# A hybrid decoder trunk: the same tiles, laid out so that the large ones begin at multiples of 1024 bytes

## The chip, the cores and the metric

The kernel runs on one core of a Trainium2 chip. The metric is the device time of one execution in microseconds (us). Before the change the median of three runs is 1990.35 us (1989.92 to 1994.62). PE is the matrix engine (PEld its weight loads), DVE the vector engine, ACT the scalar engine, POOL the GpSimd, SP the queue that issues the transfers. SBUF is the on-chip memory of 128 partitions that all tiles below live in; the matmul results go to eight banks of PSUM.

## The reference

A two-layer trunk on x (256 tokens, 2048 features), all in float32:

```python
x = recurrent_block(x, norm1_g[0], lru_w_in[0], conv, gates, lambda, lru_w_out[0])   # RMSNorm, 2048 -> 4096, conv, RG-LRU scan, 2048 -> 2048
x = swiglu_ffn(x, norm2_g[0], ffn_w_in[0], ffn_w_out[0])      # 2048 -> 2 x 5632 -> 2048
k_band, v_band = shared_kv(x, kv_norm_g, w_kv, k_norm_g)      # 4 heads of 64
x = attn_block(x, norm1_g[1], w_q[0], q_norm_g[0], sinks[0], w_o[0], k_band, v_band)   # 32 heads, window 128, sinks
x = swiglu_ffn(x, norm2_g[1], ffn_w_in[1], ffn_w_out[1])
```

All the work that counts is in the projections: some 373 MB of float32 weights are read once, each multiplied with 256 token columns.

## The kernel before, in words

**A product in three.** Every float32 operand is split into a high part (rounded to the matrix engine's fp32r format) and a low part, the rest. A product is then high x high, high x low and low x high, each an fp32r matmul. The weights are loaded from HBM in tiles of 128 x 1024 floats (512 KB) into one of four buffers `raw`, ACT copies the rounded part into `hi` (L311) and DVE subtracts it from `raw` into `lo` (L312); `hi` and `lo` have four buffers each as well. The activations x are kept transposed, and their high and low parts lie side by side in one work tile of the pool `s`, 256 high columns and then 256 low ones: a half of one of thirty 4096-byte tiles `s0` to `s29`, handed out and taken back by the class itself.

**The order of the work.** `stream` (L332) goes through a list of jobs, one for each weight tile: it issues the load of the tile four jobs ahead, splits the tile three jobs ahead, and records the matmuls of the job itself. Between the halves of a job, background tasks (norms, convolution, scan, attention, splitting of activations) are recorded as far as a budget of DVE and ACT time goes, which is kept in constants of the class and not in anything that is measured or that depends on where a tile lies.

**Which operands meet in the matrix engine.** A matmul has a stationary operand, which is loaded first (128 columns), and a moving one that is streamed through it (256 or 512 columns of 4 bytes). A profile names a matmul `out<-moving,stationary`.
- L358 (`products`), the bulk: stationary is 128 columns of `hi` or `lo`, moving 256 columns of an `s` tile (`b<-s,hi`, `b<-s,lo`). In some jobs (`sync`) a few are 512 columns wide, the high and the low part at once.
- L512 (`put`, in the groups of the feed-forward input with an odd number from 5 to 17), where pairs of products are replaced by seven products of sums: a job of `fast` has seven triples of matmuls. In three triples (9 matmuls) the moving operand is a weight tile, `hi` or `lo`, and the stationary one an activation in `s` (`b<-hi,s`, `b<-lo,s`). In the other four (12 matmuls) the moving operand is a sum of weights, made by `mix` (L314) into tiles of the pool `s`, so that both operands are in `s` (`b<-s,s`). Jobs of `plain` have moving operands in `hi` and `lo` alone.

The two lines of `fast` that say which operand is where, and the order of the triples:

```python
old = lambda q: (hi[:, q * T:q * T + T], lo[:, q * T:q * T + T])
new = lambda q: (mh[:, q * T:q * T + T], ml[:, q * T:q * T + T])
todo = ((5, part(a, 0), old(1)), (3, part(b, 0), old(3)), (2, com(3), old(2)),
        (7, com(0), new(0)), (6, com(2), new(1)), (4, com(1), new(2)), (1, part(b, 1), new(3)))
```

- L1232 (queries): stationary `s`, moving 512 columns of `hi` or `lo`. L1274: thirty matmuls on a tile of zeros at the start, while the first weights are still on their way.

**Where a tile lies.** A pool places its tiles one behind the other in the order in which they are first asked for, each rounded up to 32 bytes. `par` (1096 bytes a partition), `con` (4104) and `cc` (128) come first; x, `raw`, `hi`, `lo` and the small tiles follow, and the thirty `s` tiles, asked for last, come behind `rstd` (1032 bytes each), `acc`, `sq` and `zero`. So x, `raw`, `hi`, `lo`, `t` and `h` all begin 384 bytes past a multiple of 1024, and the `s` tiles 960 past one, that is 64 bytes short of the next. A second pool, `tmp`, holds `nm`, `nt`, `r2` and `rr`.

Of the kernel before, what the change touches and what calls it, by code (L numbers as in the profile page):

```python
# [12 lines left out]
F32 = mybir.dt.float32  # L13
F32R = mybir.dt.float32r
# [3 lines left out]
P = 128  # L18
D = 2048
T = 256  # L20
# [15 lines left out]
K_ONE, K_BLK, K_SEL0, K_SEL1, K_ID = 0, 128, 256, 384, 512  # L36
K_HS, K_MASK = 640, 642
NCON = 642 + 384


class Val:


    def __init__(self, ap=None):
        self.ap = ap
        self.ready = False


class Trunk:
# [22 lines left out]
    def __init__(self, ctx, tc, dram):  # L72
        self.tc, self.nc, self.d = tc, tc.nc, dram
        nc = self.nc
        const = ctx.enter_context(tc.tile_pool(name="const", bufs=1))
        psum = ctx.enter_context(tc.tile_pool(name="psum", bufs=1, space=bass.MemoryType.PSUM))
        tmp = ctx.enter_context(tc.tile_pool(name="tmp", bufs=1))
        self.tmp = tmp
        self.par = const.tile([P, NPAR], F32, name="par")
        self.con = const.tile([P, NCON], F32, name="con")  # L80
        self.cc = const.tile([P, 32], F32, name="cc")
        self.x = [const.tile([P, 4, T], F32, name=f"x{i}") for i in range(4)]
        self.whole = deque((i, 0) for i in range(30))
        self.stamp = 0
        self.part = {F32: deque(), F32R: deque()}
        self.spool = const
        self.held = {}
        self.raw = [const.tile([P, 1024], F32, name=f"raw{i}") for i in range(4)]
        self.hi = [const.tile([P, 1024], F32R, name=f"hi{i}") for i in range(4)]
        self.lo = [const.tile([P, 1024], F32R, name=f"lo{i}") for i in range(4)]  # L90
        self.sets = [[psum.tile([P, 512], F32, name=f"b{4 * i + j}") for j in range(4)] for i in range(2)]
        self.banks = deque(b for q in self.sets for b in q)
        self.misc = 0
        self.started = False
        self.tmps = deque(const.tile([P, T], F32, name=f"t{i}") for i in range(4))
        self.halves = deque(const.tile([P, T], F32, name=f"h{i}") for i in range(4))
        self.rstd = [const.tile([P, T + 2], F32, name=f"rstd{i}") for i in range(2)]
        self.acc = const.tile([P, T], F32, name="acc")
        self.sq = deque(const.tile([P, T], F32, name=f"sq{i}") for i in range(2))
        self.zero = const.tile([P, P + T], F32R, name="zero")  # L100
        self.jobs = []
        self.mixed = {}
        self.pend = deque()
        self.bg = deque()
        self.tick = -2 * self.LD
        self.dve = 0.0
        self.act = 0.0
# [1141 lines left out]

    def run(self):  # L1250
        nc, d = self.nc, self.d
        const = self.tmp
        self.nm = const.tile([P, T + 2], F32, name="nm")
        self.nt = const.tile([P, T + 2], F32, name="nt")
        self.r2 = const.tile([P, 2], F32, name="r2")
        self.rrs = [const.tile([P, 48], F32, name=f"rr{i}") for i in range(2)]
        self.rv = {i: Val() for i in range(4)}
        self.rstd = {0: self.rstd[0], 1: self.rstd[1], 2: self.rstd[0], 3: self.rstd[1]}
        vals = lambda: [Val() for _ in range(ND)]
        self.xs0, x1, xk, x2, x3 = (vals() for _ in range(5))  # L1260

        def first():
            for k in range(ND):
                self.gained(k, [(C_N1A, self.xs0)])
                yield 2 * (k == 1)
            for k in range(ND):
                yield from self.squares(k)
            yield from self.norm(0, self.NORM0)
            self.decay()
        self.spawn(first())  # L1270
        nc.vector.memset(self.zero[:, :].bitcast(F32), 0.0)
        p = self.bank()
        for _ in range(self.WARM):
            nc.tensor.matmul(p[:, 0:T], self.zero[:, 0:P], self.zero[:, P:P + T], start=True, stop=True)  # L1274
        self.free_bank(p)

        self.lru([(C_N2A, x1)], 1)
        self.ffn(0, x1, 1, [(C_KVG, xk)], 2, C_N2A)
        self.kv(xk, 2, [(C_N1B, x2)])
        self.attn(x2, 2, [(C_N2B, x3)], 3)  # L1280
        self.ffn(1, x3, 3, None, None, C_N2B, d["out"])
        self.stream()
# [14 lines left out]
def constants():  # L1297
    i = np.arange(P)
    con = np.zeros((P, NCON), np.float32)
    con[:, K_ONE:K_ONE + P] = 1.0  # L1300
# [46 lines left out]
```

## Time and profile before

| | us |
|---|---|
| median of 3 runs (lowest, highest) | 1990.35 (1989.92, 1994.62) |
| the profiled execution | 1994.55 |
| its span, first to last instruction | 1992.4 |
| PE busy | 1982.9 (16487 matmuls) |
| DVE busy | 1458.5 (2319 instructions) |
| ACT busy | 1123.0 (1626 instructions) |
| DMA, share of its 16 engines (weights, x, output) | 56.6% |

The profile is of one execution. The end of a matmul is modelled, and matmuls overlap, so the busy time of PE says that it never stands still, and not how fast it goes. How fast it goes is read from a count and a stretch: so many matmuls between two starts. The timeline and the chain of waits both give a start, a length and a count in each row.

### The profile page before, as it was taken

The page shows a single profiled execution, that of the slowest core. Times are in us where ns is not written, and L with a number is a line of the kernel's source. Part 1 is how long each engine was busy: PE and PEld are TensorE (multiplying, and loading weights), DVE is VectorE, ACT ScalarE, POOL GpSimd, SP SyncE. Part 2 cuts the span into 40 slices and gives each one's busy share as a digit, 9 for nine tenths or more (in the row PEclk, how much of TensorE's full clock was granted, in tenths as well). Part 3 has the DMA queues.
Part 4 walks back from the last instruction along what each step waited for, and adds up shares of the span by engine and source line. Part 5 has one row for each costly group of instructions (what it writes and reads, how often), then busy time and mean ns, then how long its engine had stood idle before and what let it go on. Part 6 is the DMA issues. An engine that isn't in the chain of part 4 may idle for free. (4 is left out here: it accounts for less than half of the span.)

```text
span 1992.4 us, 39949 instructions
## 1 busy us (share of the span) xinstructions
PE 1982.9 (100%) x16487; PEld 1935.5 (97%) x16487; DVE 1458.5 (73%) x2319; ACT 1123.0 (56%) x1626; POOL 0.2 (0%) x4
## 2 busy tenths in 40 slices
PE   9999999999999999999999999999999999999999
PEld 9999999999999999999998789999999999999999
DVE  8989868788888955555677776697888888444543
ACT  7788756555555744444556775564555556444342
POOL 0000000000000000000000000000000000000000
PEclk9999999999999999999999999999999999999999
DMA  7555655655566565555554334565655655556663
GB/s 267 194 188 180 201 191 180 202 198 194 199 201 199 196 196 197 191 191 201 192 181 154 111 128 150 189 191 190 203 201 196 198 196 197 187 190 204 208 202 128
DMA packets 105015, 376.56 MB, mean 189 GB/s; under 512 B 11648, under 2 KB 13824, under 8 KB 104832
## 3 DMA queue, kind: packets, MB, share of 16 engines
q1 hardware_dynamic: 104544, 373.60, 56.6%
q8 instruction: 129, 2.11, 0.4%
q14 instruction: 54, 0.44, 0.1%
q10 hardware_dynamic: 288, 0.40, 0.1%
HBM read 371.86 MB, written 2.10 MB: 188 GB/s over the span
## 5 line engine op out<-in xcount | busy, mean ns | idle before, releaser
L358 PE MATMUL b<-s,hi 128*128 128x256 f32 (+1 forms) x8455 | 1128.5, 280 | 1.6 <-ACT s L118 1.2
L312 DVE TENSOR_TENSOR lo<-raw,hi 128x1024 fp32r<-128x1024 f32 (+1 forms) x621 | 755.9, 1220 | 435.7 <-ACT hi L311 421.2
L358 PEld LDWEIGHTS b<-s,hi 128*128 128x128 f32 x8455 | 1051.7, 188 | 14.2 <-ACT s L118 2.0
L311 ACT ACTIVATE hi<-raw 128x1024 fp32r<-128x1024 f32 (+1 forms) x621 | 654.2, 1056 | 590.5 <-PE b L358 475.0
L358 PE MATMUL b<-s,lo 128*128 128x256 f32 x4352 | 647.1, 277 | 0.0
L358 PEld LDWEIGHTS b<-s,lo 128*128 128x128 f32 x4352 | 564.7, 188 | 0.1
L512 PE MATMUL b<-hi,s 128*128 128x256 f32 (+1 forms) x868 | 163.0, 292 | 0.0
L325 ACT ACTIVATE s<-s 128x1024 fp32r<-128x1024 f32 x84 | 89.2, 1062 | 108.6 <-DVE s L324 107.8
L512 PEld LDWEIGHTS b<-hi,s 128*128 128x128 f32 x868 | 130.4, 189 | 3.8
L512 PE MATMUL b<-s,s 128*128 128x256 f32 x1008 | 133.3, 281 | 0.0
L512 PEld LDWEIGHTS b<-s,s 128*128 128x128 f32 x1008 | 125.2, 189 | 0.0
L327 DVE TENSOR_TENSOR s<-s,s 128x1024 fp32r<-128x1024 f32 x84 | 102.7, 1222 | 20.1 <-ACT s L325 19.9
L512 PE MATMUL b<-lo,s 128*128 128x256 f32 (+1 forms) x434 | 114.1, 289 | 0.0
L118 ACT ACTIVATE s<-s 128x512 fp32r<-128x512 f32 (+3 forms) x172 | 83.0, 519 | 18.4 <-DVE s L127 13.1
L321 ACT ACTIVATE hi<-raw 128x768 fp32r<-128x768 f32 x84 | 70.3, 843 | 35.1 <-issue 21.8
L1232 PE MATMUL b<-hi,s 128*128 128x512 f32 x256 | 84.0, 408 | 0.0
L326 DVE TENSOR_TENSOR lo<-raw,hi 128x768 fp32r<-128x768 f32 x84 | 79.9, 951 | 0.0
L512 PEld LDWEIGHTS b<-lo,s 128*128 128x128 f32 x434 | 76.4, 188 | 1.8
L127 DVE TENSOR_TENSOR s<-s,s 128x512 fp32r<-128x512 f32 (+2 forms) x143 | 74.0, 549 | 4.4 <-ACT s L118 4.4
L322 DVE TENSOR_TENSOR s<-raw 128x512 f32<-128x512 f32 x84 | 57.7, 686 | 12.4 <-DMA raw<-in_ffn_in 12.3
L118 ACT ACTIVATE s<-b 128x256 fp32r<-128x256 f32 (+4 forms) x112 | 49.9, 480 | 25.9 <-PE b L1128 7.9
L1232 PEld LDWEIGHTS b<-hi,s 128*128 128x128 f32 x256 | 45.8, 189 | 9.6 <-issue 1.4
(117 smaller groups left out, 1098.6 us busy)
## 6 DMA issues: line engine op xcount, KB each, us to landing
raw<-in_ffn_in SPq DMA_DIRECT2D x352, 512.0 KB, 3.3
raw<-in_ffn_out SPq DMA_DIRECT2D x176, 512.0 KB, 3.3
raw<-in_lru_in SPq DMA_DIRECT2D x63, 512.0 KB, 3.8
raw<-in_lru_out SPq DMA_DIRECT2D x32, 512.0 KB, 3.4
raw<-in_w_q SPq DMA_DIRECT2D x32, 512.0 KB, 3.2
raw<-in_w_o SPq DMA_DIRECT2D x32, 512.0 KB, 3.3
raw<-in_gate SPq DMA_DIRECT2D x8, 512.0 KB, 4.0
raw<-in_kv SPq DMA_DIRECT2D x8, 512.0 KB, 3.2
```

What stands on the lines that cost most here:

```text
L118: self.nc.scalar.activation(out, in_, func, **kw)
L127: self.nc.vector.tensor_tensor(out, a, b, op)
L311: self.nc.scalar.activation(hi[:, q], raw[:, q], AF.Copy)
L312: self.nc.vector.tensor_tensor(lo[:, q], raw[:, q], hi[:, q].bitcast(F32), ALU.subtract)
L321: act(hi[:, q], raw[:, q], AF.Copy)
L322: tt(two(d[:, 0:2 * T]), two(raw[:, T:3 * T]), raw[:, 0:T].unsqueeze(1).to_broadcast([P, 2, T]), ALU.subtract)
L325: act(mh[:, :], d[:, :], AF.Copy)
L326: tt(lo[:, q], raw[:, q], hi[:, q].bitcast(F32), ALU.subtract)
L327: tt(ml[:, :], d[:, :], mh[:, :].bitcast(F32), ALU.subtract)
L358: self.nc.tensor.matmul(ps[f][:, 0:c1 - c0], w, x2[k][:, c0:c1], start=f not in begun, stop=last and all(q[1] != f for q in todo[n + 1:]))
L512: nc.tensor.matmul(st["ps"][b][:, h % 2 * T:(h % 2 + n) * T], x, w, start=b not in st["begun"], stop=True, skip_group_check=True)
L1232: nc.tensor.matmul(st[g][b][:, :], x, q, start=c + kt == 0 and x is xh and q is wh, stop=c == 7 and kt == 1 and q is wl)
```

## The change: the order in which the tiles are allotted

Nothing is computed differently. The small tables (`rstd`, `nm`, `nt`, `r2`, `rr`, `zero`) are asked for directly behind `par`, `con` and `cc`, then a pad of 608 bytes that nobody reads or writes, then x, `raw`, `hi`, `lo` and the work tiles, and the `s` tiles last as before. The pool `tmp` is gone, its tiles are in `const`. `acc` is now the first of three tiles of one list.

```diff
+PAD = 152
...
-        tmp = ctx.enter_context(tc.tile_pool(name="tmp", bufs=1))
-        self.tmp = tmp
...
         self.cc = const.tile([P, 32], F32, name="cc")
+        self.rstd = [const.tile([P, T + 2], F32, name=f"rstd{i}") for i in range(2)]
+        self.nm, self.nt = (const.tile([P, T + 2], F32, name=n) for n in ("nm", "nt"))
+        self.r2 = const.tile([P, 2], F32, name="r2")
+        self.rrs = [const.tile([P, 48], F32, name=f"rr{i}") for i in range(2)]
+        self.zero = const.tile([P, P + T], F32R, name="zero")
+        const.tile([P, PAD], F32, name="pad")
         self.x = [const.tile([P, 4, T], F32, name=f"x{i}") for i in range(4)]
+        self.raw = [const.tile([P, 1024], F32, name=f"raw{i}") for i in range(4)]
+        self.hi = [const.tile([P, 1024], F32R, name=f"hi{i}") for i in range(4)]
+        self.lo = [const.tile([P, 1024], F32R, name=f"lo{i}") for i in range(4)]
+        self.tmps = deque(const.tile([P, T], F32, name=f"t{i}") for i in range(4))
+        self.halves = deque(const.tile([P, T], F32, name=f"h{i}") for i in range(4))
+        self.sq = deque(const.tile([P, T], F32, name=f"sq{i}") for i in range(3))
+        self.acc = self.sq.popleft()
```

Byte addresses within a partition, and what they leave on division by 1024 and by 512:

| tiles | first address before | mod 1024 | mod 512 | first address after | mod 1024 | mod 512 |
|---|---|---|---|---|---|---|
| `x0` to `x3` | 21888 | 384 | 384 | 28672 | 0 | 0 |
| `raw0` to `raw3` | 38272 | 384 | 384 | 45056 | 0 | 0 |
| `hi0` to `hi3` | 54656 | 384 | 384 | 61440 | 0 | 0 |
| `lo0` to `lo3` | 71040 | 384 | 384 | 77824 | 0 | 0 |
| `t`, `h` (eight of 1024 bytes) | 87424 | 384 | 384 | 94208 | 0 | 0 |
| `acc`, `sq` | 97728 | 448 | 448 | 102400 | 0 | 0 |
| `s0` to `s29` | 102336 | 960 | 448 | 105472 | 0 | 0 |
| `rstd` | 95616 | 384 | 384 | 21888 | 384 | 384 |
| `zero` | 100800 | 448 | 448 | 26528 | 928 | 416 |

`par`, `con` and `cc` stay where they were. The instructions of every engine and of every queue, their order and what each waits for are the same, row for row: 10864 rows of PE, 2230 of DVE, 1513 of ACT and 715 of SP in both programs. What differs is the address in an operand, the line numbers, and the name `sq` where `acc` stood.

More of the change, by code (lines that the diff above doesn't have):

```diff
@@ L87, in __init__ @@
         self.held = {}
-        self.raw = [const.tile([P, 1024], F32, name=f"raw{i}") for i in range(4)]
-        self.hi = [const.tile([P, 1024], F32R, name=f"hi{i}") for i in range(4)]
-        self.lo = [const.tile([P, 1024], F32R, name=f"lo{i}") for i in range(4)]
         self.sets = [[psum.tile([P, 512], F32, name=f"b{4 * i + j}") for j in range(4)] for i in range(2)]
@@ L94, in __init__ @@
         self.started = False
[L95 to L100, printed above, removed]
         self.jobs = []
@@ L1251, in run @@
         nc, d = self.nc, self.d
[L1252 to L1256, printed above, removed]
         self.rv = {i: Val() for i in range(4)}
```

## The prediction

> **What bounds the kernel now.** I read the page's busy times first, then what the matrix engine waits for, then the chain of waits.
>
> ```profile
> PE 1982.9 (100%) x16487; PEld 1935.5 (97%) x16487; DVE 1458.5 (73%) x2319; ACT 1123.0 (56%) x1626; POOL 0.2 (0%) x4
> ...
> PE b L463 <- DVE acc L127: 1.7, 1, 1.7
> PE b L1274 <- DVE zero L1271: 1.3, 1, 1.3
> PE b L358 <- ACT s L118: 1.2, 2, 0.8
> ...
> core 0: 1992.4 us, clock 1.000
> ```
>
> PE is never without work: its three longest waits come to 4.2 us of a span of 1992.4, at a full granted clock. DVE and ACT are idle for a quarter and for nearly a half of it. So the time is 16487 matmuls one behind the other, and only the distance from one matmul to the next can move it. The mean length of a matmul is modelled and says little about that distance; a piece of the chain of waits has a length and a count.
>
> ```profile
> 1403.73 21.76 PE b L358 x192
> 1425.49 7.41 PE b L512 x63
> ```
>
> Columns: start, length, what, how many. These two stand one behind the other, with the same shape (256 moving columns). The first takes 21.76 / 192 = 113.3 ns a matmul, the second 7.41 / 63 = 117.6 ns. The second is three jobs of `fast`, each with 9 matmuls whose moving operand is `hi` or `lo` and 12 whose operands are both in `s`. The timeline takes them apart:
>
> ```profile
> 538.37 1.59 PE L512 MATMUL b<-s,s 128*128 128x256 f32 x12
> 539.80 0.40 PE L512 MATMUL b<-hi,s 128*128 128x256 f32 x2
> ...
> 540.84 1.58 PE L512 MATMUL b<-s,s 128*128 128x256 f32 x12
> 542.26 0.40 PE L512 MATMUL b<-hi,s 128*128 128x256 f32 x2
> ```
>
> From the first start to the second, 12 matmuls with both operands in `s` take 1.43 us, 119.2 ns each; from the second to the third, the 9 with `hi` and `lo` take 1.04 us, 115.6 ns (some of them still come out of the slower stretch); then again 12 in 1.42 us, 118.3 ns. Within one job, at one shape, nothing differs but where the moving operand lies. An `s` tile begins 448 bytes past a multiple of 512, and `hi` and `lo` 384. All slices that the matmuls take begin at multiples of 512 bytes within a tile. So `s` against `hi` is always 64 bytes apart on division by 512, and `s` against `s` is 0 apart. The pairs that are 0 apart are the slow ones.
>
> There is a second thing to see. The same stage, the last projection, runs at two speeds:
>
> ```profile
> 162.00:211.00 49.00, 48.91 (x412) 1.00 0.56 187
> 1208.00:1234.00 26.00, 26.00 (x216) 1.00 0.54 179
> 1670.00:1750.00 80.00, 80.00 (x674) 1.00 0.57 188
> 1760.00:1840.00 80.00, 80.00 (x696) 1.00 0.61 199
> ```
>
> Columns: stretch, its length, PE busy with its count, granted clock, DMA share, GB/s. With the same mixture of 256 and 512 columns, 80 us hold 674 matmuls (118.7 ns) up to 1750 and 696 (114.9 ns) from 1760 on, at the same clock. The distance has two levels and keeps one for tens of us. The stretches at 162 and 1208 are on the slow one too (118.7 and 120.4 ns). The three slow rows hold 412 + 216 + 674 = 1302 matmuls; with the start and shorter stretches, read in the same way, I count some 2,000 on the slow level.
>
> **The change part by part.** It adds and removes no instruction, moves none and adds no wait. Only addresses change, so each part is a class of operands.
>
> *Matmuls between `s` and `hi` or `lo`.* After the change all of these tiles begin at multiples of 512 bytes, so every such pair is 0 apart, as today only the `s`,`s` pairs are.
>
> ```profile
> L358 PE MATMUL b<-s,hi 128*128 128x256 f32 x8206 | 1080.8, 277 | 1.4 <-ACT s L118 1.2
> L358 PE MATMUL b<-s,lo 128*128 128x256 f32 x4352 | 647.1, 277 | 0.0
> L512 PE MATMUL b<-hi,s 128*128 128x256 f32 x784 | 140.2, 279 | 0.0
> L512 PE MATMUL b<-lo,s 128*128 128x256 f32 x392 | 97.6, 278 | 0.0
> L512 PE MATMUL b<-s,s 128*128 128x256 f32 x1008 | 133.3, 281 | 0.0
> ```
>
> The first four rows have 8206 + 4352 + 784 + 392 = 13734 matmuls. What would one cost at distance 0? From the chain's row, with 115.6 ns for the 27 others, the 36 `s`,`s` matmuls take (7410 - 27 x 115.6) / 36 = 119.1 ns; the timeline's two runs say 119.2 and 118.3. I take 119.1, 5.8 ns over the 113.3 of the fast level. Some 11,700 matmuls are on that level now: 11,700 x 5.8 = 68 us. The 2,000 on the slow level, some 118 ns, lose about 1 ns each: 2 us. Together 70 us. Bounds: the least is the step from the fast to the slow level, 118.7 - 114.9 = 3.8 ns, 11,700 x 3.8 = 44 us. The most is 113.3 for the 27 others as well, which leaves (7410 - 27 x 113.3) / 36 = 120.9 ns for `s`,`s`: 7.6 x 11,700 + 2.9 x 2,000 = 95 us.
>
> *Matmuls with both operands in `s`*: the distance stays 0, so 1008 at the same price, nothing. Below nothing only if the place within 512 bytes matters and not the distance; that is a rival.
>
> *512 moving columns.*
>
> ```profile
> L1232 PE MATMUL b<-hi,s 128*128 128x512 f32 x256 | 84.0, 408 | 0.0
> L358 PE MATMUL b<-s,hi 128*128 128x512 f32 x249 | 71.7, 394 | 0.1
> L1232 PE MATMUL b<-lo,s 128*128 128x512 f32 x128 | 50.8, 397 | 0.0
> ```
>
> No row has such a matmul at distance 0. Its weight load is as long as that of a narrow one, so I bound its loss by nothing and 7.6 ns: 633 of them, 0 to 5 us. I take 0: what they lose, if anything, is small beside the bounds of the narrow ones.
>
> *DVE and ACT.* `raw`, `hi` and `lo` lie 0 apart today already, as do two `s` tiles.
>
> ```profile
> L312 DVE TENSOR_TENSOR lo<-raw,hi 128x1024 fp32r<-128x1024 f32 x619 | 754.5, 1222 | 431.8 <-ACT hi L311 417.4 <-PE b L512 11.1
> L327 DVE TENSOR_TENSOR s<-s,s 128x1024 fp32r<-128x1024 f32 x84 | 102.7, 1222 | 20.1 <-ACT s L325 19.9
> ```
>
> The same subtraction takes 1222 ns at 384 past 1024 and at 960 past it. So nothing is expected, and 534 us of idle time on DVE hide what there might be; a slower PE makes that cover larger.
>
> *The transfers into `raw`* now land at multiples of 1024.
>
> ```profile
> raw<-in_ffn_in SPq DMA_DIRECT2D x352, 512.0 KB, 3.3
> ...
> DVE s L322 <- DMA raw<-in_ffn_in: 12.3, 16, 1.3
> ```
>
> A tile lands 3.3 us after its issue and is loaded four jobs ahead, with a job some 24 x 113 ns = 2.7 us long. DVE waits 12.3 us for them in all, off the path, and PE's waits name none. Priced at nothing either way; without the cover, 12.3 us.
>
> Sum: 1994.55 + 70 = 2065 us for the profiled execution. That one was 4.2 us above the median of the runs, so 2060 us against the median. Bounds 44 and 95, with 5 for the wide ones: 2034 to 2090.
>
> [...] The rows above have the 63 matmuls of L512 at 117.6 ns beside 192 of L358 at 113.3. [...]
>
> **The rivals.**
> *Nothing happens.* Loads and streams don't meet, and `s`,`s` is slow in L512 for another reason, for instance since each of these matmuls writes a quarter of another bank than the triple ahead of it. Against: the triples on `hi` and `lo` in the same jobs change banks as well, at 115.6 ns. For: the two levels of L358 at one and the same distance show that something other than the distance acts too. The time stays at 1990, 1986 to 1996 by the spread of the runs. That the tiles would not be where the change says is excluded by their addresses, all of them multiples of 1024.
>
> *It gets faster.* Not the distance counts but the place: a 512-byte piece that begins at 448 lies across a multiple of 512, and where both operands do so, as in `s`,`s`, the engine pays. After the change no piece lies across one. Its place is every matmul with an `s` operand, and it decides from the point where the cost is that of crossing. Then 1008 `s`,`s` gain 119.1 - 113.3 = 5.8 ns, 6 us, and if the slow level goes as well, 2,000 x 5 ns = 10 us: 1990 - 16 = 1974 us. Against it: L358 streams its moving operand across such multiples at 113.3 ns, and the `hi`,`s` matmuls load theirs across them, without a cost that the rows show.
>
> *Between.* The two levels remain, and pairs 0 apart share their time between 113 and 119 ns: half of the 70 us, 2025.
>
> **How the numbers follow.** The forecast, 2060 us, has 0.68, and 2034 to 2090 for itself. Nothing happens 0.12, faster 0.13, between 0.07. 0.3% of 1990 is 6 us, about what a measurement of this kernel can tell from no change. The range goes down to 1986, so that "nothing" and "between" are in it, and up to 2086. Left out are the faster case and the last few us above, about 0.16. Faster 0.13, same 0.12, slower 0.75.
>
> **What would show it.** If right: PE busy throughout as before, the rows of L358 that had 192 matmuls in 21.76 us have them in 22.7 to 23.2, L512's 63 in about 7.5, and the windows of the last projection show one level near 119 ns or above. The length of a DVE subtraction stays at 1222 ns. The prediction is wrong if L358 stays at 113.3 ns with all tiles at multiples of 1024, or if L512's 63 fall to 7.1 us: then it was not the distance. If it gets slower with PE idle, something else has come in.

## The result and the profile after

The changed kernel takes 2070.32 us (median of 4 runs, 2070.28 to 2070.69) against 1990.18 us (median of 4, 1989.92 to 1994.62): a ratio of 1.0398, 95% interval 1.038 to 1.0416. The forecast was 2060 us.

The page of the changed kernel, its first row, and what PE waited for (us in total, times, longest):

```profile
PE 2060.5 (100%) x16487; PEld 2015.7 (97%) x16487; DVE 1462.9 (71%) x2319; ACT 1127.8 (55%) x1626; POOL 0.2 (0%) x4
```

```profile
PE b L1272 <- DVE zero L1269: 1.3, 1, 1.3
PE b L1131 <- DVE s L139: 1.1, 3, 0.4
PE b L1086 <- ACT s L121: 0.7, 1, 0.7
```

PE has as many matmuls as before, never stands still, and waits for even less: these three, its longest, come to 3.1 us, and the three longest of before to 4.2. It is busy for 77.6 us more, with the same instructions. The line numbers have shifted: L361 is the L358 of before, L515 the L512. The chain of waits (start, length, what, count), first of the changed kernel:

```profile
1454.00 23.04 PE b L361 x192
1477.04 7.56 PE b L515 x63
...
1728.53 336.57 PE b L361 x2772
```

and the last projection in the kernel before:

```profile
1667.78 321.60 PE b L358 x2772
```

The 192 matmuls that took 113.3 ns each take 23.04 / 192 = 120.0 ns. The 63 of L515 take 7.56 / 63 = 120.0 ns, the same: the triples on `hi` and `lo` and those with both operands in `s` can't be told apart any more. The last projection is 15.0 us longer. The timeline of a job of `fast` shows it by itself:

```profile
1522.21 1.60 PE L515 MATMUL b<-s,s 128*128 128x256 f32 x12
1523.65 0.40 PE L515 MATMUL b<-hi,s 128*128 128x256 f32 x2
```

From one start to the next, 1.44 / 12 = 120.0 ns. And where the last projection had two levels within one stage, there is one:

```profile
1730.00:1810.00 80.00, 80.00 (x664) 1.00 0.56 184
1820.00:1900.00 80.00, 80.00 (x658) 1.00 0.58 191
```

664 and 658 matmuls in 80 us at a full granted clock (column 4), where it was 674 and 696. The second stretch has fewer only because it holds more wide matmuls, 12 against 6; over the whole kernel the narrow ones of L361 are 120.2 ns apart. It fits this that the runs of the changed kernel lie within 0.4 us and those of before within 5: no second level shows in its trace, where the mean of 17 neighbours is 120.0 ns in the median and at least 117.3 throughout; in that of before it is 113.4 in the median and some 118 on the slow level. DVE and the transfers, from the groups, the waits and the issues:

```profile
L315 DVE TENSOR_TENSOR lo<-raw,hi 128x1024 fp32r<-128x1024 f32 x619 | 756.2, 1224 | 503.1 <-ACT hi L314 499.2
```

```profile
raw<-in_ffn_in SPq DMA_DIRECT2D x352, 512.0 KB, 3.3
```

The subtraction takes 1224 ns (1222 before), a tile of weights still lands in 3.3 us. All of the difference is in PE.

### The profile page after: what moved, and what is told of

It reads as the page before. It is cut to its first block, busy times and chain, and to the rows that moved or that the text cites. A ratio compares the mean times of both kernels' runs of the same rounds, so it can differ in the third digit from the quotient of the medians.

```text
span 2068.1 us, 39949 instructions
## 1 busy us (share of the span) xinstructions
PE 2060.5 (100%) x16487; PEld 2015.7 (97%) x16487; DVE 1462.9 (71%) x2319; ACT 1127.8 (55%) x1626; POOL 0.2 (0%) x4
## 4 chain that ended last, share of the span: by engine, by line
PE 97%; ACT 1%; DVE 1%; DMA 1%; issue 0%; SPq 0%; ACTq 0%
PE b L361 74%; PE b L515 14%; PE b L1235 4%; PE b L850 1%; ACT s L121 1%; PE b L1086 1%; PE b L1150 1%; PE b L1041 1%; PE b L1131 1%; ACT hi L314 0%; DMA x<-in_x 0%; PE b L714 0%; PE b L1209 0%; DMA raw<-in_lru_in 0%; PE b L1051 0%
## 5 line engine op out<-in xcount | busy, mean ns | idle before, releaser
L361 PE MATMUL b<-s,hi 128*128 128x256 f32 (+1 forms) x8455 | 1178.2, 286 | 0.7 <-ACT s L121 0.5
L315 DVE TENSOR_TENSOR lo<-raw,hi 128x1024 fp32r<-128x1024 f32 (+1 forms) x621 | 757.6, 1222 | 507.1 <-ACT hi L314 503.1
L361 PEld LDWEIGHTS b<-s,hi 128*128 128x128 f32 x8455 | 1097.8, 192 | 12.6 <-ACT s L121 0.7
L361 PE MATMUL b<-s,lo 128*128 128x256 f32 x4352 | 673.2, 283 | 0.0
L361 PEld LDWEIGHTS b<-s,lo 128*128 128x128 f32 x4352 | 588.9, 192 | 0.1
L515 PE MATMUL b<-hi,s 128*128 128x256 f32 (+1 forms) x868 | 166.1, 294 | 0.0
L515 PEld LDWEIGHTS b<-hi,s 128*128 128x128 f32 x868 | 132.6, 191 | 3.8
L515 PE MATMUL b<-s,s 128*128 128x256 f32 x1008 | 134.6, 283 | 0.0
L515 PEld LDWEIGHTS b<-s,s 128*128 128x128 f32 x1008 | 127.0, 192 | 0.0
L515 PE MATMUL b<-lo,s 128*128 128x256 f32 (+1 forms) x434 | 116.1, 294 | 0.0
L515 PEld LDWEIGHTS b<-lo,s 128*128 128x128 f32 x434 | 77.9, 191 | 1.7
```

Source lines behind the costliest of these rows:

```text
L315: self.nc.vector.tensor_tensor(lo[:, q], raw[:, q], hi[:, q].bitcast(F32), ALU.subtract)
L361: self.nc.tensor.matmul(ps[f][:, 0:c1 - c0], w, x2[k][:, c0:c1], start=f not in begun, stop=last and all(q[1] != f for q in todo[n + 1:]))
L515: nc.tensor.matmul(st["ps"][b][:, h % 2 * T:(h % 2 + n) * T], x, w, start=b not in st["begun"], stop=True, skip_group_check=True)
```

## The experiments

### Is it the distance or the place?

The first run puts 64 bytes ahead of the `s` tiles of the changed kernel; everything else stays at multiples of 1024.

```diff
         self.acc = self.sq.popleft()
+        const.tile([P, 16], F32, name="gap")
```

> The kernel after, with 64 bytes ahead of the s tiles: x, raw, hi, lo, t, h still begin at multiples of 1024, the s tiles 64 bytes past one, so s against hi is 64 bytes apart again. Theory of the distance (both operands read at the same address on division by 512 cost): back to 1990 us, 1985 to 1997, 192 matmuls of L361 in about 21.8 us, most matmuls at 113 ns and some stretches at 118. Rival of the place (operands or transfers at multiples of 1024 cost): hi, lo, raw and x are there still, so 2040 to 2070 us.

Measured: 1990.26 us (1989.68 to 1991.95), ratio to before 0.9995 (0.9986 to 1.0004). Its chain:

```profile
1402.71 21.76 PE b L362 x192
1424.47 7.41 PE b L516 x63
...
1666.68 318.54 PE b L362 x2772
```

The two pieces have the lengths of before to the last digit. The last projection is 3.1 us shorter than in the profile of before (318.54 against 321.60), of 4.2 us between the two profiled executions (1990.40 and 1994.55). Counted from the starts in the traces (the mean of 17 neighbours between 117 and 118.3 ns), 1,249 of the narrow matmuls of that line are near 118 ns here and 1,947 in the profile of before: most of what two executions at distance 64 differ by is the time that they spend on the slow level. The second run takes the kernel before and puts 448 bytes there, so that no tile lies at a multiple of 512 but `s` and `hi` leave the same rest.

```diff
         self.zero = const.tile([P, P + T], F32R, name="zero")
+        const.tile([P, 112], F32, name="gap")
```

> The kernel before, with 448 bytes ahead of the s tiles: nothing begins at a multiple of 1024, but s and hi both 384 bytes past one, distance 0. Theory of the distance: 2070 us, 2064 to 2076, one level of 120 ns. Rival of the place: 1990 us, since not one tile lies at a multiple of 512 or 1024.

Measured: 2070.46 us, ratio 1.0397 (1.0378 to 1.0415), the time of the changed kernel within 0.2 us.

```profile
1454.05 23.04 PE b L359 x192
1477.09 7.56 PE b L513 x63
```

So the multiples of 1024 cost nothing and bring nothing here: 1990.26 us with them and 1990.26 before, at distance 64; 2070.32 with them and 2070.46 without, at distance 0. What the change did was to make the distance between `s` and the weight buffers zero. The rival of the place, in both directions, falls, and so does the one that nothing happens.

### Matmuls alone, one distance after the other

> Matmuls alone; the kernel computes nothing of the reference and copies x to the output. Sixteen cases, one moving tile each (da to dp): 24 matmuls at distance 0, 64 of 256 columns at the case's distance, 4 of 512 columns, 64 of 256 again. Distances in bytes: da 0, db 16, dc 32, dd 64, de 96, df 128, dg 192, dh 256, di 320, dj 384, dk 448, dl 4; dm and dn are 0 and 64 with both operands moved on by 64 bytes, do and dp the same by 160. No transfer and no other engine runs beside them. Theory of the distance: da, dm and do 120 ns a matmul, dd, dn and dp 113 or 118, alike whatever the place; between distances somewhere a step, and if a distance goes below 113 it is a better layout. Rival of the place: da, dm and do differ from one another. A rival that other engines' or transfers' reads are the cause: no case differs from another, and all are below 113.

The kernel has one weight tile and sixteen moving ones. By its program ACT does nothing but fill them, and DVE and the queues nothing but bring x in and copy it to the output; in the second kernel of bare matmuls, further down, the DMA share is 0.00 to 0.01 in the six stretches of 6 us that were read. From the timeline (start, length up to the modelled end of the last matmul, count):

```profile
74.97 16.16 PE L46 MATMUL b<-dd,w 128*128 128x256 f32 x132
90.97 3.04 PE L46 MATMUL b<-da,w 128*128 128x256 f32 x24
...
132.01 15.62 PE L46 MATMUL b<-dg,w 128*128 128x256 f32 x132
147.47 3.02 PE L46 MATMUL b<-da,w 128*128 128x256 f32 x24
150.33 16.44 PE L46 MATMUL b<-dh,w 128*128 128x256 f32 x132
166.60 3.04 PE L46 MATMUL b<-da,w 128*128 128x256 f32 x24
```

The row names the shape of the 128 narrow matmuls; four wide ones, some 0.93 us by the 232.5 to 233.4 ns apiece that the last kernel of bare matmuls gives at 64, 128 and 192, are in the count. From a case's start to the next row's, less 0.93, divided by 128: 117.7 ns at distance 64 (dd), 113.5 at 192 (dg), 119.8 at 256 (dh). By the same reckoning:

| distance, bytes | 0 (dm, do) | 4 | 16 | 32 | 64 | 96 | 128 | 192 | 256 | 320 | 384 | 448 |
|---|---|---|---|---|---|---|---|---|---|---|---|---|
| ns per matmul | 119.8 | 123.2 | 117.7 | 117.2 | 117.7 | 120.0 | 118.7 | 113.5 | 119.8 | 117.7 | 118.7 | 113.5 |

Each figure is a mean of two stretches of 64 matmuls, one ahead of the four wide ones and one behind them. By the starts of the single matmuls the two are alike but at 16 bytes, 118.7 ns ahead and 116.6 behind, and at 32, 117.8 and 116.7: a first sign that one distance can have two levels.

256, 320, 384 and 448 repeat 0, 64, 128 and 192, so what counts in these cases is the distance modulo 256, not 512 as the prediction had it. Moving both operands on by 64 or by 160 bytes changes nothing: 119.8 ns again at distance 0 (dm, do), 117.7 at 64 (dn). The levels show without the work that the other engines and the queues do in the big kernel. None of these distances goes below 113.3 ns.

### Two more distances in the kernel

Gaps of 48 and of 32 floats in the place of the 16 in the first diff.

> The kernel after, with 128 bytes ahead of the s tiles. Theory of the distance, by m1's 118.7 ns at 128: some 13,700 matmuls gain 1.3 ns on the 120 of after, 18 us, so 2052 us, 2045 to 2058. A theory in which only distance 0 costs, and all else is as before: 1990 us.

Measured: 2054.91 us, ratio 1.0316 (1.0302 to 1.033), as expected from the bare matmuls.

```profile
1444.72 22.79 PE b L362 x192
1467.51 7.50 PE b L516 x63
```

22.79 / 192 = 118.7 ns, the very figure of the bare matmuls at 128.

> The kernel after, with 192 bytes ahead of the s tiles, so that s lies 192 past hi and lo. The bare matmuls of m1 ran at 113.3 ns at 192 whatever was ahead of them, and at 117.8 at 64. Theory of the distance: L361 has one level of 113.3 ns, 192 of them always in 21.76 us, and the 2,000 slow ones of before gain 4.7 ns each, 9 us; the 1,176 matmuls of L515 with hi or lo moving come to lie at 64 and lose up to 4.5 ns, 5 us. So 1981 to 1986 us, below both kernels. If the slow level of before came from something else than the distance (a stall, the transfers), it is still there: 1988 to 1992.

Measured: 2028.48 us, ratio 1.0188 (1.0174 to 1.0202). This is a miss: over 40 us above the range that I expected, and above the rival's too.

```profile
1641.09 21.77 PE b L362 x192
1662.86 7.47 PE b L516 x63
...
1692.48 330.48 PE b L362 x2772
```

The 192 behind the fast groups have 113.4 ns, but the last projection is 8.9 us longer than before, with its narrow matmuls at some 118 ns. So 192 has two levels as well as 64, and the kernel fell into the upper one for most of the projections: 8,905 of the 12,557 narrow matmuls of L362, counted as above.

### What chooses the level

The projections have a few wide matmuls in some jobs (three, one behind the other, where `sync` says so), the feed-forward input behind the fast groups has none. A kernel of bare matmuls, now in the order of L361, with three and then four wide ones between stretches of 60:

> Matmuls alone again, nothing of the reference is computed. Twelve distances (da 0, db 48, dc 64, dd 80, de 160, df 176, dg 188, dh 192, di 196, dj 208, dk 224, dl 240), now in the order of L361: four weight slices with a high and a low moving half each, then four low slices; 24 matmuls at distance 0, 60 at the case's, 3 wide, 60, 4 wide, 60. If the order of the operands or an odd number of wide ones lets a stretch at 64 take the fast level, dc shows 113 after the 3 wide ones and 118 ahead of them; if not, dc stays at 118 throughout and the two levels need another cause. For 192 the theory of the distance says 113.3 throughout; near it either a broad valley of 113 or a single point, and below 113 if there is a better distance.

Pieces of the timeline within the three stretches at 64 (dc) and at 192 (dh):

```profile
70.92 6.64 PE L40 MATMUL b<-dc,w 128*128 128x256 f32 x55
...
78.79 6.40 PE L40 MATMUL b<-dc,w 128*128 128x256 f32 x55
...
86.64 6.52 PE L40 MATMUL b<-dc,w 128*128 128x256 f32 x54
...
200.26 6.40 PE L40 MATMUL b<-dh,w 128*128 128x256 f32 x55
...
207.77 6.41 PE L40 MATMUL b<-dh,w 128*128 128x256 f32 x53
...
215.41 6.64 PE L40 MATMUL b<-dh,w 128*128 128x256 f32 x55
```

A piece's length less 0.28 us, the length that the timeline gives a single matmul of this shape, divided by its count less one. At 64: 117.8 ns, behind three wide ones 113.3, behind four 117.7. At 192: 113.3, behind three wide ones 117.9, and behind four it stays there, 117.8. In the kernel of sixteen cases four wide ones had changed neither: 64 stayed at 117.8, 192 at 113.3. So what stands ahead has a part in the level, but a rule that says which number of wide ones leads where does not come out of these cases. Distance 0 shows no second level (119.8 to 120.0 throughout). 80 has one, 120.0 ns, behind three wide ones 118.3 and behind four 120.0 again; the others have none here: 48 has 118.4, 160 has 117.4, 176 and 188 have 119.2 and 119.4, 196 has 120.4, 208 has 119.1, 224 has 118.3 and 240 has 117.2 ns. Of the distances tried, 113.3 ns is not a valley but two points, 64 and 192.

If the wide ones choose, then taking them out of the projections must turn the two distances round. Both runs have this edit beside their gap, of 16 floats for 64 bytes and of 48 for 192:

```diff
-    SYNC = (0, 2, 5)
+    SYNC = ()
...
-                self.group(src, ND, xn, direct, g == NH // 2 - 1, (0, 3, 4, 5) if end else (), True, 3 if end else None)
+                self.group(src, ND, xn, direct, g == NH // 2 - 1, (), True, 3 if end else None)
```

> The same without wide matmuls in L361, but at distance 64. By the theory of the levels, in m2 the tile at 64 was at 117.8 ns until three wide ones had gone by; without them it stays there from the start and from each stall on: 2015 to 2045 us, most of L361 at 118 ns. Rival, that at 64 the fast level is simply the rule: 1985 to 1992 us.

Measured: 2024.65 us, ratio 1.0155 (1.0135 to 1.0174). The last projection, of 2808 matmuls now that each wide one is two narrow ones:

```profile
1687.57 330.74 PE b L362 x2808
```

330.74 / 2808 = 117.8 ns, the upper level throughout. In the next expectation, "the run before" is the one at 192 with the wide ones in.

> Distance 192 as in the run before, and no job of L361 has wide matmuls any more (SYNC is empty, nor has the group behind the last fast one any): 256 columns throughout but for L515 and the queries. Theory that a pair of operands has a set of levels by its distance, and what stands ahead chooses among them: in m2 the tile at 192 took 113.3 ns behind narrow matmuls at distance 0 and 118 behind wide ones, so L361 now has 113.3 ns nearly throughout, and the 2028 us of the run before become 1976 to 1986, below both kernels. Rival: the wide ones don't choose the level, it drifts or comes from stalls: 2020 to 2035 us.

```profile
1634.73 7.47 PE b L516 x63
...
1664.32 318.27 PE b L362 x2808
```

318.27 / 2808 = 113.3 ns, the lower one throughout. The same edit gives the opposite at the two distances. Counted as above over all narrow matmuls of the line, the upper level has 1,947 of 12,557 at 64 with the wide ones (the kernel before) and 8,963 of 13,055 without; at 192 it has 8,905 with them and 335 without. So the wide ones have a part in it. They are not all: the 192 matmuls behind the fast groups took the lower level, 21.76 and 21.77 us, in these two runs as in the two with the wide ones.

In time the run was a miss: 1993.58 us (1987.43 to 1995.86) where 1976 to 1986 was expected, ratio to before 0.9991 (0.9978 to 1.0005), no difference that I can tell. Four of the twelve runs lie between 1987.4 and 1987.7, eight between 1991.4 and 1995.9; the profile is of the first kind. Part of the miss is my count: the 2,000 slow matmuls of before are those of an execution of 1994.55 us, 4 us above the median that I subtracted from; the profile of the run with 64 bytes, at 1990.40, has some 1,300. Against 1994.55, 1987.47 is 7 us less, where 2,000 x 4.7 ns = 9 us were counted for the slow level. Why eight runs are longer is open, as there is no profile of one of them.

### The pairs that are both in s

Four of the thirty tiles, 26 to 29, come from a pool of their own that begins with a gap of 192 bytes more. The sums of weights take one of them where one is free; everything else takes one only where no other is free.

```diff
+        self.mpool = ctx.enter_context(tc.tile_pool(name="mix", bufs=1))
+        self.mpool.tile([P, 48], F32, name="gap2")
...
-        i, _ = self.whole.popleft()
-        s = self.spool.tile([P, 4 * T], dt, tag=f"s{i}", name=f"s{i}")
+        k = next((k for k, q in enumerate(self.whole) if (q[0] >= 26) == mix), 0)
+        i = self.whole[k][0]
+        del self.whole[k]
+        s = (self.mpool if i >= 26 else self.spool).tile([P, 4 * T], dt, tag=f"s{i}", name=f"s{i}")
...
-        mh, ml = self.double(), self.double()
+        mh, ml = self.double(mix=True), self.double(mix=True)
```

> As the run without wide ones at 192, and the sums of weights of L515 go, where one is free, into four of the thirty tiles that lie another 192 bytes on, so that the 1008 matmuls with both operands in s are 192 apart too and not 0. Theory of the distance: they go from 120 to 113 or 118 ns, so another 2 to 7 us below the run without: 1970 to 1984. Rival: something else of these matmuls costs, no change against that run.

Measured: 1999.76 us, ratio to before 1.0028 (1.0015 to 1.0042): not below the run ahead of it but 6 us above.

```profile
1402.93 21.91 PE b L366 x192
1424.84 7.44 PE b L520 x63
```

The 63 gained 0.03 us. By the addresses of their tiles, 560 of the 1,008 pairs came to lie at 192, and those took 117.8 ns; the rest got no tile of the four. And where the four tiles held activations, L366 read them 384 from `hi`, which is 128 modulo 256: 648 matmuls at 118.8 ns that were near 113.3. That is not the larger part of the loss. Between the two profiles, 1987.47 and 1994.91 us, the narrow matmuls of L366 lost 8.4 us, of which these 648 account for some 3.5; most of the rest is that the matmuls still at 192 stayed longer on the upper level, some 1,900 of them against some 400 in the run without the four tiles. Whether the mixed distances ahead sent them there was not tested. So no version here beats both kernels.

### Which pair is it?

> Bare matmuls again, nothing of the reference is computed; each case has 24 at distance 0 and 96 of its own. Which pair of operands counts: a moving operand and its own weights, or a moving operand and the weights of the next matmul, which are loaded beside it? The weights move on with each matmul in steps, so that the two distances differ. Own distance, then next, in bytes modulo 256: da 0 and 0, db 0 and 192, dc 64 and 0, dd 192 and 0, de 0 and 128, df 128 and 0. Theory of the next load: dc, dd and df 120 ns as da, db 113 or 118, de 118.7. Rival of the own weights: db and de 120, dc and dd 113 or 118, df 118.7. [...]

```profile
31.82 11.54 PE L44 MATMUL b<-db,w 128*128 128x256 f32 x96
...
46.07 11.46 PE L44 MATMUL b<-dc,w 128*128 128x256 f32 x96
...
60.25 11.52 PE L44 MATMUL b<-dd,w 128*128 128x256 f32 x96
...
102.62 11.05 PE L44 MATMUL b<-dg,w 128*64 128x256 f32 x96
...
116.38 11.47 PE L44 MATMUL b<-dh,w 128*32 128x256 f32 x96
...
130.57 21.94 PE L44 MATMUL b<-di,w 128*128 128x512 f32 x96
...
155.22 22.57 PE L44 MATMUL b<-dj,w 128*128 128x512 f32 x96
```

dg and dh have weights of 64 and 32 columns instead of 128, at distance 0; di, dj, dk and dl have 512 moving columns at distance 0, 64, 192 and 128. Lengths less 0.28 us, over 95: db 118.5, dc 117.7, dd 118.3 ns, and de and df 116.7, with 120.0 for da. None of them stays at 120, neither the ones whose own distance is 0 nor the ones whose next is. So neither theory of the pair holds by itself, and which pair it is stays open. In the other runs of bare matmuls, and within a stretch of L358, both distances are the same modulo 256, so there one number stands for both. The price doesn't follow the weights' columns either: at distance 0, 128 columns take 120.0 ns, 64 take 113.4 and 32 take 117.8. With 512 moving columns, from one case's start to the next row's, distance 0 takes 226.9 ns, 64 and 192 take 233.4, and 128, from the starts, 232.5: there, zero is the best of the four, which I had not expected at all.

## Why the prediction was right, step by step

*PE alone sets the time, at a distance per matmul and not by waits*: right. From the starts of the matmuls in the two traces, the 12,557 narrow ones of L358 that have a successor add up to 1438.4 us before and 1509.3 after, 70.9 more; the narrow ones of L512 on `hi` and `lo` to 136.1 and 140.7, 4.6 more; those with both operands in `s` to 119.7 and 121.0, 1.3 more; the wide ones to 183.0 and 182.2. The sum, 76 us, is within 0.4 us of the difference of the two profiled executions, 2070.28 - 1994.55 = 75.7.

*The `s`,`s` rows of before as a sample of what all pairs would do*: right, and shown by moving the distance alone in both directions. The period was taken too large, 512 for 256 bytes, which changed nothing here. What it could not see is that 64 bytes is no ordinary place: the pairs that are not 0 apart were fast because 64 is one of the two distances, of all that were tried, that reach 113.3 ns. In L512, where `hi` or `lo` moves and `s` is stationary, the same 64 bytes counted the other way are 192 modulo 256, which is the other one.

*The price*: the term that was mis-sized, twice. I took 119.1 ns from rows in which each run of 12 comes out of a faster stretch and needs a few matmuls to settle: over the 84 runs of 12 in the trace of before, the first eight steps are 118.0 ns on average, the last four 120.0. The settled figure is 120.0, as the 192 in a row show: 11,700 x (120.0 - 113.3) = 78 us for 68, and 2,000 x (120.0 - 118) = 4 for 2. With that the sum is 82, above the 76 measured. The larger part of what it is over is in the 1,176 matmuls of L512 on `hi` and `lo`. The sum has them on the level of 113.3 ns, although the prediction itself had read 115.6 for such ones. They took 136.1 us / 1,176 = 115.8 ns before and 119.7 after, so they lost 4.6 us and not 1,176 x 6.7 ns = 7.9. Another 2.3 us are in gaps of over 140 ns between matmuls of L358, which the kernel after has fewer of. The price was too low and the count of fast matmuls too high; that the forecast is only 10 us off is in part the luck of two errors that go against each other.

*The two levels*: read rightly as a second thing that acts. That the changed kernel would have one level was forecast, and with it falls the rival in which both levels stay; why before has two was not known. What stands ahead has a part in it (bare matmuls at 64: 117.8 ns, 113.3 behind three wide ones, 117.7 behind four), by a rule that is still open.

*512 columns and the `s`,`s` pairs at nothing*: right within 1.3 us. *DVE, ACT and the transfers at nothing*: right, with 1224 ns a subtraction for 1222, 1058 ns for ACT's copy into `hi` in both, and 3.3 us from issue to landing in both.

*That an address can matter at all*: the time did not stay at 1990 us but went to 2070, and the bare matmuls, with hardly anything else going on, took 113.5 to 123.2 ns by the distance of their two operands alone. What in the engine makes it so is not shown; that the addresses of the two operands, taken together, have a part in the pace is.

## What to carry to other kernels

Where a matrix engine is busy throughout, count matmuls between two starts, by operand, and compare kinds that stand in the same job: in the rows of before, the busy time (100%) and the modelled mean length (277 and 281 ns) hide a difference of 5% (113.3 against 119.2 ns from start to start). An alignment to a round number was no gain in itself here (1990.26 us with it and without it at distance 64); what counted was how far the moving operand lies from the stationary one modulo 256 bytes, and aligning all tiles alike set that to 0, one of the slower values for 256 moving columns (120.0 ns; 113.3 at the fastest). Before tuning such a distance, look at whether its best value has two levels: at 64 and 192 bytes it had, 113.3 and 117.8 ns, and the matmuls ahead had a say in which one a stretch got.

## What was not expected of the hardware

A stream of fp32r matmuls of 128 weight columns and 256 moving ones settles at 113.3 to 123.2 ns at a full granted clock, depending on the distance of the operands modulo 256 bytes, and can hold its level for hundreds of matmuls: 2,808 of them at 113.3 ns at distance 192, and as many at 117.8 at 64, in the last projection without wide ones. In this kernel the levels were 113.3, 117.8, 118.7 and 120.0. At 64 and 192 bytes there are two levels, 113.3 and 117.8, and three wide matmuls moved a stretch of bare matmuls from one to the other; 16, 32 and 80 have two as well, closer together (118.7 and 116.6, 117.8 and 116.7, 120.0 and 118.3). With 512 moving columns the order is turned round, 226.9 ns at distance 0 and 233.4 at 64 and 192. What inside the chip makes it so was not found; that at distance 0 weights of 128 columns run at 120.0 ns, of 64 at 113.4 and of 32 at 117.8 speaks against a cost that simply grows with the columns loaded.
